# A decoder trunk on one core: the dense stage waits for 96 sums of the second gathered tile, and the first two tiles keep the old row ring

## The chip, the cores and the metric

The kernel runs on one core of a Trainium2 chip. A core has five engines, each working through its own list of instructions in order: TensorE (PE in the profile) multiplies matrices, VectorE (DVE) and ScalarE (ACT) work element by element, GpSimd (POOL) issues the indirect DMAs here, SyncE (SP) issues the plain ones. An instruction that has to wait holds up all that stands behind it on its engine. The metric is the time of one execution on the device in microseconds, lower is better. The kernel before takes 3243.36 us, the median of three runs (3237.42 to 3247.24).

## The reference

The kernel computes one layer of a decoder trunk for 1024 prompt tokens and 32 sample tokens (8 sequences of 4) of width 1024, all in float32. First come mixers (a matrix memory, a spatial gating, a pooling) with a projection in, a projection out and a layer norm. The part that this case is about is the feed-forward that follows, a PEER layer: each token picks 8 heads x 16 of 16384 experts, and each expert is one row of `peer_u` and one row of `peer_v`:

```
s1, i1 = top_k(scores[:, :, 0], 16); s2, i2 = top_k(scores[:, :, 1], 16)
top_s, top_pos = top_k(s1[..., :, None] + s2[..., None, :], 16)   # of 256 pairs, per head
g = softmax(top_s)
act  = gelu(einsum('nd,nhkd->nhk', x2, peer_u[idx]))     # 128 rows of 1024 per token
out  = einsum('nhk,nhkd->nd', g * act, peer_v[idx])      # 128 rows of 1024 per token
y = layer_norm(ALPHA * x1 + g2 * out) * ln2_g + ln2_b
```

## The kernel before, in words

The 1024 prompt tokens are eight tiles of 128, numbered 0 to 7, and the sample tokens are a ninth, numbered 8 (`NT`). They take two ways through the PEER layer.

**Gathered tiles** are 0, 1, 6, 7 and the sample (`GATHERED`, 544 tokens' worth of steps: 4 x 128 and 32). For each step GpSimd issues one indirect DMA (`gather`, L1267 to L1272) that brings 128 rows of 1024 floats, one to a partition, 0.524 MB. `u_items` does this with `peer_u`: the rows of the k-th expert of all 128 tokens, which VectorE multiplies with x2 and sums into a column of `sv` (L1297, in the text also "product"). The index is cast on VectorE from the choice of the experts, 16 columns at a time (L1293, `ii`). After 128 products `finish` makes the coefficients (`cT_`) and the transposed indices (`iT`). `v_items` then does one token per step: its 128 rows of `peer_v` are multiplied on TensorE with an expanded coefficient column (`cexp`, VectorE L1344, one per eight tokens, in a ring of two) and go into a PSUM tile `acc` (L1354; in the text a "sum"; a pair of tokens is eight matmuls in the trace). After a tile's last token comes its finish: `finish_tile` (L1434) before the dense stage, `g_finish` (L1408) in it.

The rows land in two rings of six slots: `rows` from the start, `rows2` for `peer_v` as soon as that scope exists. `rows2` is opened when the text of the dense stage begins, in memory that the scopes `build` and `front` give back (L1476 to L1483).

**Dense tiles** are 2 to 5 (`DENSE`). They compute all 16384 experts for 512 tokens. In the build stage `g_weights` turns the chosen experts into a table: VectorE makes pair tables `ab` (L1041 to L1044, ring of two), ScalarE scales six columns of each (L1046), TensorE multiplies them (`pgm`, L1053), ScalarE copies the result (`gs`, L1056), and SyncE writes it to memory (`G_d`, L1060). `g_pre` beside it does 32 of the 128 score chunks ahead of time. Then the dense stage (`g_dense`, L1095) walks the experts: 24 matmuls `psd` (L1066) for each of the 96 remaining chunks, and 256 groups of 12 matmuls `po` (L1173). ScalarE and VectorE split each incoming table into two half-precision parts (`us`, L1119 and L1120; `vs`, L1136 and L1137), make the coefficients (`act`, `coef`, L1156 to L1164) and add up the outputs (`acc`, L1182).

**What sets the order.** The text of the kernel is produced by generators (`g_main`, `g_gates`, `g_pre`, `g_gather`, and so on), which `run` (L107) takes in turn by rough costs that each yield gives; a generator can wait for a key, such as `("weights", t)` or `"chosen"`, which another adds to `ready`. `g_main` waits for the tables, the choices and the pre-scores before it opens the dense stage (L1471 to L1477). Instructions also carry a priority, gathers a higher one (`AHEAD_S`, `AHEAD_U`, `AHEAD_V`), and a scheduler that simulates the program fixes from text and priorities the order of each engine's list. On the chip only these lists and the semaphores between them count. `g_gather` (L1565) alternates between the `peer_u` steps of one tile and the `peer_v` steps of the tile before it.

Of the kernel before, what the change touches and what calls it, by code (L numbers as in the profile page):

```python
# [44 lines left out]
)  # L45
NROW = 6
NROW2 = 6
MB = 2.78
GATHERED = (0, 1, 6, 7, NT)
DENSE = (2, 3, 4, 5)  # L50
# [27 lines left out]
def kernel(ctx: ExitStack, tc: tile.TileContext, A, O):  # L78
# [236 lines left out]
    ready = set()  # L315
# [948 lines left out]
                            channel_multiplier=0)  # L1264
    coef = {}

    def gather(table, idx):  # L1267
        own = table == "peer_v" and "rows2" in cur
        s = cur["rows2" if own else "rows"].tile("row", (P, D), F32, NROW2 if own else NROW)
        nc.gpsimd.indirect_dma_start(out=s[:], out_offset=None, in_=A[table],  # L1270
                                     in_offset=bass.IndirectOffsetOnAxis(ap=idx, axis=0))
        return s  # L1272
# [51 lines left out]
    def v_items(t):  # L1324


        smp = t == NT
        cT_, iT = coef[t]
        pv = [psum.tile([P, 512], F32, name=f"acc{e}", tag=f"acc{e}", bufs=1) for e in range(2)]
        nj = 8 if smp else 32  # L1330
        hold = {}
        for j in range(nj):
            for q in range(4):

                def step(j=j, q=q):
                    if j % 2 == 0 and q == 0:
                        ce_ = hold["c"] = cur["rows"].tile("cexp", [P, 2, 4, 32], F32, 2)
                        if smp:
                            cv = cT_[:, 4 * j:4 * j + 8].rearrange("p (j q) -> p j q", q=4)
                            dv = delta[:, :, 32 - 4 * j:64 - 4 * j].rearrange("p (j q) c -> p j q c", q=4)  # L1340
                        else:
                            cv = cT_.rearrange("p (q j) -> p j q", q=4)[:, j:j + 2, :]
                            dv = delta[:, 0:2, 32 - j:64 - j].unsqueeze(2).to_broadcast([P, 2, 4, 32])
                        V.tensor_tensor(out=ce_, in0=cv.unsqueeze(3).to_broadcast([P, 2, 4, 32]), in1=dv, op=ALU.mult)  # L1344
                    tok = 4 * j + q if smp else 32 * q + j
                    hold[q % 2] = gather("peer_v", iT[:, tok:tok + 1]), hold["c"][:, j % 2, q, :]
                    if q % 2 == 0:
                        return lambda: None
                    rows = hold[0], hold[1]

                    def add(b, e):
                        g = 32 * (q - 1 + b ^ 2 * e)
                        s, l = rows[b]
                        return mm(pv[e][g:g + 32, :], lhsT=l, rhs=s[:, e * 512:e * 512 + 512], start=(j == 0),  # L1354
                                  stop=(j == nj - 1), skip_group_check=True)

                    def use():
                        first = add(1, 0)
                        with tc.issue_after(first.ins):
                            add(1, 1)  # L1360
                            add(0, 0)
                            add(0, 1)
                    return use
                yield step

        def finish():
            src = pv
            if smp:
                src = []
                f = cur["rows"].tile("row", (P, D), F32, NROW)  # L1370
                fs = [f[:, 0:512], f[:, 512:1024]]
                for e in range(2):
                    (S.activation(fs[e], pv[e], AF.Copy) if e else V.tensor_copy(fs[e], pv[e]))
                yield 0, 1.2, 0
                for e in range(2):
                    b = bank("pfold")
                    mm(b[:NS], lhsT=fold, rhs=fs[e], start=True, stop=True)
                    src.append(b)
                yield 1.8, 0, 0
            if R:  # L1380
                yield from g_finish(t, NS if smp else P, src)
            else:
                finish_tile(t, NS if smp else P, src)
        yield finish
# [78 lines left out]
    def g_main():  # L1463
        yield from g_ada(0)
        load_consts()
        for ts in PASSES:
            yield from g_first(ts)
        cur["proj"].close()
        cur["build"] = Scope("build")
        ready.add("build")  # L1470
        for t in DENSE:  # L1471
            yield from wait(("weights", t))
        yield from wait("chosen")
        yield from wait("pre")
        for t in (NT - 1, NT):
            yield from wait(("y", t, 0))  # L1476
        flush(0)  # L1477
        cur["build"].close()
        cur["front"].close()
        ready.add("dense")  # L1480
        cur["dense"] = Scope("dense")
        dense = g_dense(cur["dense"])
        cur["rows2"] = Scope("rows2", "right")  # L1483
        cur["fin"] = Scope("fin2")
        load_rows()
        yield from dense
# [76 lines left out]
    def g_gather():  # L1563
# [6 lines left out]
        while todo or us or vs or done:  # L1570
            if us is None and todo and (todo[0], 0) in ready and len(done) < 2:
                t = todo.pop(0)
                us, iu = list(u_items(t)), 0
                nu = len(us) - 1
            if vs is None and done:
                vs, iv = list(v_items(done[0])), 0
                nv = len(vs) - 1
            need = None
            if us:
                need = ("routed", t) if iu == nu else (t, 7 if t == NT else iu // 16)  # L1580
            if us and need in ready and (not vs or iu * nv <= 1.4 * (iv - HOLD.get(t, 0) * nv) * nu):
                if iu == nu:
                    flush(0)
                    sooner(AHEAD_F, us[-1])
                    us = None
                    done.append(t)
                    continue
                pend.append((AHEAD_U, sooner(AHEAD_S, us[iu])))
                iu += 1
                c = 0, 1.14, 1.46  # L1590
            elif vs:
                if iv == nv:
                    flush(0)
                    end = vs[-1]()
                    while (x := sooner(AHEAD_F, lambda: next(end, None))):
                        yield x
                    vs = None
                    done.pop(0)
                    continue
                if R and iv >= nv - 24 and iv % 4 == 0:  # L1600
                    if iv == nv - 24:
                        soon = g_ahead(done[0])
                    next(soon, None)
                pend.append((AHEAD_V, sooner(AHEAD_S, vs[iv])))
                iv += 1
                c = 0.43, 0, 1.46
            else:
                yield from wait(need or (todo[0], 0))
                continue
            flush(LAG)  # L1610
            yield c
# [111 lines left out]
```

## Time and profile before

| | |
|---|---|
| median of three runs | 3243.36 us (3237.42 to 3247.24) |
| the profiled execution | 3252.89 us, span 3251.2 us |
| mean granted TensorE clock | 0.902 of full speed |
| TensorE busy | 2748.0 us, 85% of the span |
| VectorE busy | 2202.4 us, 68% |
| GpSimd busy | 1293.1 us, 40% |
| ScalarE busy | 929.6 us, 29% |
| moved by DMA | 962.24 MB, mean 296 GB/s |

Times in the trace count from the start of the span. The busy share of an engine is an average over stages of different kinds. The stretches that the text uses are: the front of the kernel to 1143 us; the last projections and choices to 1360; the build stage to 1668; the dense stage from 1676 to 3092, when the last `po` group is through; and the last gathers to the end.

### The profile page before, as it was taken

How to read it: one execution, taken by the hardware profiler on the slowest of the kernel's cores; microseconds unless marked ns; L12 is line 12 of the kernel's file. 1: busy time of each engine (PE TensorE's matmuls, PEld its weight loads, DVE VectorE, ACT ScalarE, POOL GpSimd, SP SyncE). 2: the span in 40 equal slices, each digit the busy share in tenths (PEclk: the TensorE clock that was granted, in tenths of full speed). 3: DMA queues.
4: the chain of work that ended last, by engine and by line, in shares of the span. 5: the costliest groups of instructions: out<-in, count | busy, mean ns of one | idle time of the engine just before them, and what ended most of it. 6: DMA issues, size and time to landing. Idle time of an engine off the chain costs nothing.

```text
span 3251.2 us, 44766 instructions
## 1 busy us (share of the span) xinstructions
PE 2748.0 (85%) x16366; PEld 1410.6 (43%) x16366; DVE 2202.4 (68%) x5756; ACT 929.6 (29%) x1618; POOL 1293.1 (40%) x1096
## 2 busy tenths in 40 slices
PE   6888984487976888987479999999999998999955
PEld 3447952344654366753343344333344343334300
DVE  2443998867688669777644687777677787777622
ACT  3413243112111124445762222222222222222100
POOL 0000366545445400000013555756465665554564
PEclk8988997687978999989679999999999999999955
DMA  8744798899998844423558999999899999999897
GB/s 296 245 174 138 284 345 292 292 325 312 323 333 291 318 162 141 153 84 137 209 222 317 384 390 353 383 356 399 307 389 368 391 388 363 369 354 353 298 344 257
DMA packets 368993, 962.24 MB, mean 296 GB/s; under 512 B 36757, under 2 KB 114708, under 8 KB 364668
## 3 DMA queue, kind: packets, MB, share of 16 engines
q0 software_dynamic: 156672, 570.49, 47.3%
q1 hardware_dynamic: 212100, 388.89, 34.3%
q8 instruction: 128, 2.10, 0.3%
q14 instruction: 93, 0.76, 0.1%
HBM read 890.30 MB, written 69.02 MB: 295 GB/s over the span
## 4 chain that ended last, share of the span: by engine, by line
PE 50%; DVE 12%; DMA 11%; ACT 4%; issue 3%; POOL 1%; SPq 0%; POOLq 0%; ACTq 0%; DVEq 0%
PE po L1173 18%; PE psd L1066 16%; PE acc L1354 6%; PE pqr L880 4%; DMA row<-in_peer_v,iT 4%; DMA v<-in_peer_v 3%; PE py L808 2%; DVE row L1297 2%; ACT gs L1056 1%; DMA row<-in_peer_u,ii 1%; POOL row L1270 1%; DMA G_d<-gs 1%; DMA wo<-in_w_o 1%; ACT ab L1046 1%; DVE us L1084 1%
## 5 line engine op out<-in xcount | busy, mean ns | idle before, releaser
L1270 POOL DMA_INDIRECT row<-in_peer_v,iT x544 | 631.2, 1160 | 1140.8 <-DVE us L1120 549.0
L1270 POOL DMA_INDIRECT row<-in_peer_u,ii x544 | 659.6, 1212 | 759.6 <-DVE ii L1293 315.9
L1066 PE MATMUL psd<-xd,us 128*128 128x512 f16 x3072 | 719.2, 385 | 29.9 <-ACT us L1083 22.2
L1173 PE MATMUL po<-vs,coef 128*128 128x512 f16 x3072 | 707.8, 380 | 32.2 <-ACT vs L1136 27.1
L1297 DVE SCALAR_TENSOR_TENSOR row<-row,x2u 128x1024 f32<-128x1024 f32 x544 | 656.1, 1216 | 103.2 <-DMA row<-in_peer_u,ii 89.7
L1173 PEld LDWEIGHTS <-coef 128*128 128x128 f16 x3072 | 291.3, 98 | 470.0 <-issue 127.3
L1066 PEld LDWEIGHTS <-us 128*128 128x128 f16 x3072 | 297.4, 99 | 432.0 <-issue 69.9
L1354 PE MATMUL acc<-row,cexp 128*32 128x512 f32 x2176 | 341.8, 690 | 119.2 <-DMA row<-in_peer_v,iT 106.3
L880 PE MATMUL pqr<-x2T,wpq 128*128 128x128 f32 (+1 forms) x2304 | 284.5, 284 | 2.5 <-DVE CT_s L711 0.9
L880 PEld LDWEIGHTS pqr<-x2T,wpq 128*128 128x128 f32 x2304 | 277.2, 200 | 9.0 <-DVE CT_s L711 1.7
L1182 DVE SCALAR_TENSOR_TENSOR acc<-po,scale,acc 128x512 f32<-128x512 f32 x248 | 182.9, 747 | 99.2 <-PE po L1173 90.3
L1156 ACT ACTIVATE act<-psd,scale 128x512 f32<-128x512 f32 x96 | 65.8, 685 | 617.3 <-PE psd L1066 524.8
L1158 DVE SCALAR_TENSOR_TENSOR act<-act,scale,g 128x512 f32<-128x512 f32 x128 | 96.1, 751 | 164.9 <-ACT act L1156 135.1
L1137 DVE SCALAR_TENSOR_TENSOR vs<-v,vs 128x1024 f16<-128x1024 f32 x128 | 155.6, 1219 | 56.6 <-ACT vs L1136 47.6
L1354 PEld LDWEIGHTS acc<-row,cexp 128*32 128x32 f32 x2176 | 48.3, 114 | 292.8 <-DMA row<-in_peer_v,iT 161.2
L1136 ACT ACTIVATE vs<-v 128x1024 f16<-128x1024 f32 x128 | 132.5, 1047 | 142.9 <-DMA v<-in_peer_v 117.8
L1053 PE MATMUL pgm<-ab 128*128 128x128 f16 x1024 | 98.9, 253 | 83.2 <-DVE ab L1043 43.9
L808 PE MATMUL py<-wo,Y 128*128 128x512 f32 (+1 forms) x288 | 144.6, 653 | 21.4 <-DMA wo<-in_w_o 12.4
L1120 DVE SCALAR_TENSOR_TENSOR us<-u,us 128x1024 f16<-128x1024 f32 x96 | 117.3, 1222 | 46.9 <-ACT us L1119 45.3
L1163 ACT ACTIVATE coef<-act 128x512 f16<-128x512 f32 x128 | 79.8, 624 | 201.9 <-DVE act L1158 174.7
L1056 ACT ACTIVATE gs<-pgm 128x256 f32<-128x256 f32 x256 | 124.1, 633 | 40.8 <-PE pgm L1053 25.6
L279 PEld LDWEIGHTS <-w 128*128 128x128 f16 x2160 | 123.1, 100 | 24.8 <-issue 21.7
(337 smaller groups left out, 2856.6 us busy)
## 6 DMA issues: line engine op xcount, KB each, us to landing
v<-in_peer_v SPq DMA_DIRECT2D x128, 512.0 KB
u<-in_peer_uT SPq DMA_DIRECT2D x96, 512.0 KB
wpq<-in_w_pq SPq DMA_DIRECT2D x64, 512.0 KB
G_d<-gs SPq DMA_DIRECT2D x32, 1024.0 KB
g<-G_d SPq DMA_DIRECT2D x32, 1024.0 KB
wada<-in_w_ada SPq DMA_DIRECT2D x48, 512.0 KB
wf<-in_w_in SPq DMA_DIRECT2D x44, 512.0 KB
wo<-in_w_o SPq DMA_DIRECT2D x32, 512.0 KB
```

The costliest lines, as they stand in the source:

```text
L279: mm(out, lhsT=x if cs is None else y, rhs=y if cs is None else x, start=(i + k == 0), stop=(i == len(ps) - 1 and k == KD - 1))
L808: mm(py[t, e][:ns[t]], lhsT=Y_[t][:, k + j, :ns[t]], rhs=w[:, j, :], start=(k + j == 0), stop=(k + j == KD - 1))
L880: mm(pq[:, i * P:i * P + ns[t]], lhsT=w[:, k, :], rhs=X2[t][:, k, :ns[t]], start=(k == 0), stop=(k == KD - 1))
L1056: S.activation(gs[e][:, :, t0:t0 + 4].rearrange("p c t -> p t c"), pg[:, :, 64 * e:64 * e + 64], AF.Copy)
L1066: mm(ps, lhsT=us[a][:, k, :], rhs=xd[:, :, b, k, :], start=(m == 0), stop=(m == 23))
L1136: S.activation(vs[:, 0], v, AF.Copy, scale=SV)
L1137: V.scalar_tensor_tensor(out=vs[:, 1], in0=v, scalar=SV, in1=vs[:, 0], op0=ALU.mult, op1=ALU.subtract)
L1173: mm(po, lhsT=d[:, a, i * P:(i + 1) * P], rhs=vs[:, b, c % 2, :], start=(m == 0), stop=(m == 3 * GROUP - 1))
L1182: V.scalar_tensor_tensor(out=a, in0=po, scalar=scale[:, 3:4], in1=a, op0=ALU.mult, op1=ALU.add)
L1270: nc.gpsimd.indirect_dma_start(out=s[:], out_offset=None, in_=A[table], in_offset=bass.IndirectOffsetOnAxis(ap=idx, axis=0))
L1297: V.scalar_tensor_tensor(out=s, in0=s, scalar=1.0, in1=x2, op0=ALU.mult, op1=ALU.mult, accum_out=sv[:, k:k + 1])
L1354: return mm(pv[e][g:g + 32, :], lhsT=l, rhs=s[:, e * 512:e * 512 + 512], start=(j == 0), stop=(j == nj - 1), skip_group_check=True)
```

## The change

A constant `AMPLE` is added. The generator of the main text waits for one more key, `"ample"`, before it opens the dense stage; `g_gather` adds the key when it has put 96 steps of tile 1's `peer_v` into the text. `gather` no longer looks whether `rows2` is open: the caller says which ring it wants, and the `peer_v` rows of tiles 0 and 1 go to `rows`, those of 6, 7 and the sample to `rows2`.

```
@@ -45,6 +45,7 @@
 NROW = 6
 NROW2 = 6
+AMPLE = 96
 MB = 2.78
@@ -1264,8 +1265,7 @@
-    def gather(table, idx):
-        own = table == "peer_v" and "rows2" in cur
+    def gather(table, idx, own=False):
         s = cur["rows2" if own else "rows"].tile("row", (P, D), F32, NROW2 if own else NROW)
         nc.gpsimd.indirect_dma_start(out=s[:], out_offset=None, in_=A[table],
                                      in_offset=bass.IndirectOffsetOnAxis(ap=idx, axis=0))
@@ -1343,7 +1343,7 @@
-                    hold[q % 2] = gather("peer_v", iT[:, tok:tok + 1]), hold["c"][:, j % 2, q, :]
+                    hold[q % 2] = gather("peer_v", iT[:, tok:tok + 1], t not in GATHERED[:2]), hold["c"][:, j % 2, q, :]
@@ -1472,6 +1472,7 @@
             yield from wait(("weights", t))
         yield from wait("chosen")
         yield from wait("pre")
+        yield from wait("ample")
         for t in (NT - 1, NT):
             yield from wait(("y", t, 0))
@@ -1603,6 +1604,8 @@
                 pend.append((AHEAD_V, sooner(AHEAD_S, vs[iv])))
                 iv += 1
+                if done[0] == GATHERED[1] and iv == AMPLE:
+                    ready.add("ample")
                 c = 0.43, 0, 1.46
```

In the lists the change moves instructions at three places. Line numbers of the changed kernel are higher by one from L49 to L1266.

The first is GpSimd's list after the 256th `peer_u` step, the last of tile 1. Before, the rest of tile 0's `peer_v` rows follow, then a run of `peer_u` and `peer_v` rows in fives:

```order
L1270 DMA row<-in_peer_v,iT 128x1024
L1270 DMA row<-in_peer_u,ii 128x1024 x6
L1270 DMA row<-in_peer_v,iT 128x1024 x45
L1270 DMA row<-in_peer_u,ii 128x1024 x5
L1270 DMA row<-in_peer_v,iT 128x1024 x5
```

In the changed kernel 37 rows end tile 0 (its 128th), and the next `peer_u` row is tile 6's first:

```order
L1270 DMA row<-in_peer_u,ii 128x1024 x2
L1270 DMA row<-in_peer_v,iT 128x1024 x37
L1270 DMA row<-in_peer_u,ii 128x1024
L1270 DMA row<-in_peer_v,iT 128x1024
L1270 DMA row<-in_peer_u,ii 128x1024
L1270 DMA row<-in_peer_v,iT 128x1024
```

Behind it the rows of tile 6's `peer_u` and of tile 1's `peer_v` alternate.

The second is VectorE's list in the last third of the build stage. Before, the pair tables stand by themselves:

```order
L1041 TENSOR_TENSOR ab<-iota_106,fx 128x2048
L1042 TENSOR_TENSOR ab<-iota_106,fx 128x2048
L1043 TENSOR_TENSOR ab<-ab,fx 128x2048 x2
L1044 TENSOR_TENSOR ab<-ab,fx 128x1280 x2
L1041 TENSOR_TENSOR ab<-iota_106,fx 128x2048
L1042 TENSOR_TENSOR ab<-iota_106,fx 128x2048
```

In the changed kernel the products of tile 6 (L1297) stand between them:

```order
L1297 SCALAR_TENSOR_TENSOR row,sv<-row,x2u 128x1024
L1044 TENSOR_TENSOR ab<-ab,fx 128x2048
L1138 SCALAR_TENSOR_TENSOR vs<-v,vs 128x1024
L1297 SCALAR_TENSOR_TENSOR row,sv<-row,x2u 128x1024 x2
L1045 TENSOR_TENSOR ab<-ab,fx 128x1280
L1297 SCALAR_TENSOR_TENSOR row,sv<-row,x2u 128x1024
L1042 TENSOR_TENSOR ab<-iota_106,fx 128x2048
L1043 TENSOR_TENSOR ab<-iota_106,fx 128x2048
```

There are 79 such products between the cast of tile 6's first index and the last pair table, where before there was none.

The third is VectorE's list where the last gathered sums stand. Before, that is behind everything of the dense tiles; the first two rows end the last dense tile:

```order
L360 TENSOR_TENSOR mv<-vy,vy_25117 128x1
L785 SCALAR_TENSOR_TENSOR acc_14544<-acc_14544,mv,r_ln_b 128x1024
L1344 TENSOR_TENSOR cexp<-cT__23093,delta 128x256 x4
L1344 TENSOR_TENSOR cexp<-cT__25294,delta 128x256 x2
L1420 TENSOR_TENSOR row<-row,r_g_14531 128x1024
```

In the changed kernel it is inside the dense stage, behind the 187th of the 256 `po` groups:

```order
L1121 SCALAR_TENSOR_TENSOR us<-u,us 128x1024
L1165 TENSOR_TENSOR coef<-act,coef 128x512
L1183 SCALAR_TENSOR_TENSOR acc_15617<-po,scale,acc_15617 128x512
L1344 TENSOR_TENSOR cexp<-cT__19789,delta 128x256 x8
L1344 TENSOR_TENSOR cexp<-cT__22401,delta 128x256 x2
L1420 TENSOR_TENSOR row<-row,r_g_15605 128x1024
```

Ten `cexp` in a row, each for eight tokens, take the place of six, and 69 `po` groups come behind them. TensorE's list has 106 tokens' sums in one piece there; before it had 88 behind the last `po` group.

## Rows read from the trace of the kernel before

**Rows 1.** The page, parts 1 and 2: busy time; busy tenths in 40 slices.

```profile
PE 2748.0 (85%) x16366; PEld 1410.6 (43%) x16366; DVE 2202.4 (68%) x5756; ACT 929.6 (29%) x1618; POOL 1293.1 (40%) x1096
...
PE   6888984487976888987479999999999998999955
...
POOL 0000366545445400000013555756465665554564
```

**Rows 2.** The waits of GpSimd: us in total, times, longest.

```profile
POOL row L1270 <- DVE us L1120: 549.0, 1, 549.0
```

**Rows 3.** Timeline of GpSimd: start, us, instruction, idle before and releaser.

```profile
1135.53 0.94 POOL L1270 DMA_INDIRECT row<-in_peer_u,ii  x1 [1.39 <-DVE row L1297]
1685.46 0.94 POOL L1270 DMA_INDIRECT row<-in_peer_v,iT  x1 [548.99 <-DVE us L1120]
1686.70 0.94 POOL L1270 DMA_INDIRECT row<-in_peer_v,iT  x1 [0.30 <-issue]
```

**Rows 4.** Windows by stage: header, then busy time of each engine.

```profile
core 0: us, PE busy (x) PEld busy (x) DVE busy (x) ACT busy (x) POOL busy (x), PEclk, DMA share, GB/s
1143.00:1360.00 217.00, 196.36 (x1396) 148.65 (x1394) 167.30 (x773) 81.58 (x168) 0.00 (x0) 0.95 0.43 147
1360.00:1545.00 185.00, 149.31 (x1013) 92.30 (x1012) 134.94 (x570) 87.88 (x172) 0.00 (x0) 0.95 0.33 117
1545.00:1668.00 123.00, 60.18 (x554) 50.65 (x551) 81.20 (x89) 93.25 (x236) 0.00 (x0) 0.64 0.48 185
1676.00:3092.00 1416.00, 1376.81 (x6856) 546.05 (x6854) 1004.97 (x1474) 377.41 (x491) 790.49 (x661) 0.99 0.98 362
3092.00:3251.00 159.00, 85.92 (x356) 9.72 (x356) 39.65 (x116) 2.38 (x4) 83.23 (x83) 0.54 0.84 301
```

**Rows 5.** Waits of TensorE, the first of 1685 to 3095, the second of 3092 to 3251.

```profile
PE po L1173 <- ACT vs L1136: 27.1, 12, 4.3
...
PE acc L1354 <- DMA row<-in_peer_v,iT: 58.9, 42, 4.0
```

**Rows 6.** Timeline of TensorE: dense stage, a pair of tokens, the ends.

```profile
1675.96 16.32 PE L1066 MATMUL psd<-xd,us 128*128 128x512 f16 x72
...
1701.50 1.07 PE L1354 MATMUL acc<-row,cexp 128*32 128x512 f32 x8
...
3090.58 1.25 PE L1173 MATMUL po<-vs,coef 128*128 128x512 f16 x5
...
3233.25 1.93 PE L1354 MATMUL acc<-row,cexp 128*32 128x512 f32 x8 [1.94 <-DMA row<-in_peer_v,iT]
```

**Rows 7.** Windows with gathers beside choosing, beside projections, and alone; columns as in group 4.

```profile
350.00:500.00 150.00, 137.16 (x1300) 99.72 (x1298) 141.21 (x471) 57.83 (x89) 87.06 (x67) 0.97 0.96 349
700.00:1136.00 436.00, 351.19 (x2110) 214.59 (x2108) 329.07 (x1267) 68.79 (x153) 212.66 (x182) 0.86 0.90 315
3100.00:3230.00 130.00, 75.85 (x316) 8.48 (x320) 22.36 (x67) 1.78 (x3) 77.86 (x79) 0.52 0.95 341
```

**Rows 8.** Tile 6's index casts on VectorE: shortest, median, longest ns; first, last start.

```profile
L1293 DVE CAST ii<-rt x4: 168/168/176, 1360.2 to 1360.4; 128x16 int32<-128x16 f32 x4
```

**Rows 9.** Timeline of VectorE: `cexp`, two products, a half-row operation.

```profile
1138.33 0.42 DVE L1344 TENSOR_TENSOR cexp<-cT__6780,delta 128x256 f32<-128x256 f32 x1
...
1140.91 1.22 DVE L1297 SCALAR_TENSOR_TENSOR row<-row,x2u 128x1024 f32<-128x1024 f32 x1
...
1142.18 1.23 DVE L1297 SCALAR_TENSOR_TENSOR row<-row,x2u 128x1024 f32<-128x1024 f32 x1
...
1152.07 0.69 DVE L816 TENSOR_TENSOR z<-py,g 128x512 f32<-128x512 f32 x1 [6.73 <-PE py L808]
```

**Rows 10.** TensorE in the dense stage, of `acc`, `psd` and `po` in this order.

```profile
1676.00:3092.00 1416.00, 197.08 (x1472) 0.99 0.98 362
...
1676.00:3092.00 1416.00, 539.68 (x2304) 0.99 0.98 362
...
1676.00:3092.00 1416.00, 707.82 (x3072) 0.99 0.98 362
```

More of the change, by code (lines that the diff above doesn't have):

```diff
@@ L47 @@
 NROW2 = 6
+AMPLE = 96
 MB = 2.78
@@ L1265, with gather @@
     coef = {}
-    def gather(table, idx):
-        own = table == "peer_v" and "rows2" in cur
+    def gather(table, idx, own=False):
         s = cur["rows2" if own else "rows"].tile("row", (P, D), F32, NROW2 if own else NROW)
@@ L1345, in step @@
                     tok = 4 * j + q if smp else 32 * q + j
-                    hold[q % 2] = gather("peer_v", iT[:, tok:tok + 1]), hold["c"][:, j % 2, q, :]
+                    hold[q % 2] = gather("peer_v", iT[:, tok:tok + 1], t not in GATHERED[:2]), hold["c"][:, j % 2, q, :]
                     if q % 2 == 0:
@@ L1474, in g_main @@
         yield from wait("pre")
+        yield from wait("ample")
         for t in (NT - 1, NT):
@@ L1605, in g_gather @@
                 iv += 1
+                if done[0] == GATHERED[1] and iv == AMPLE:
+                    ready.add("ample")
                 c = 0.43, 0, 1.46
```

## The prediction

> **What bounds the kernel now.** The page's first two parts come first. TensorE is busy 85% of the span and its digits are 8 and 9 almost to the end, while GpSimd shows eight zeros in mid-kernel, so whole gathers are being held back there [rows 1]. The waits of GpSimd name the hole: one wait of 549.0 us [rows 2]. The timeline gives its place: the last row of `peer_u` for tile 1 is issued at 1135.53, the next row, one of `peer_v`, at 1685.46, with the start of the dense stage [rows 3]. The row is tile 0's 89th; it has to go into the new ring `rows2`, whose memory becomes free only there. So 88 of 544 `peer_v` rows and 256 of 544 `peer_u` rows are behind us when the dense stage begins.
>
> The windows cut the rest into stages [rows 4]: 1143 to 1360 is paced by TensorE (196.4 of 217 us busy), 1360 to 1668 by VectorE (134.9 of 185 us) and by the chain through ScalarE (93.3 of 123 us), 1676 to 3092 by TensorE (1376.8 of 1416 us), and from 3092 nothing but rows for the last sums is left. There TensorE waits 58.9 us for landings [rows 5]. The last 88 tokens take from 3092 to 3235 [rows 6], 143 us or 1.62 us each; then 16 us of finishing.
>
> **The change, part by part.** The sum is made against the profiled span, 3251.2 us (its run took 3252.9). The median of the three runs is 3243.4, so a result in profile time is multiplied by 0.997.
>
> *Until 1143 us: nothing.* Every engine's order is word for word the same until token 89's sum.
>
> *1143 to 1360: +10 us.* Tokens 89 to 128 of tile 0 now use the old ring and go at once. Their 40 sums stand among the projections. Two tokens take 1.07 us [rows 6], so 40 take 21 us on an engine with 20.6 us idle in the stretch. Between 0 and 21 I take the middle. The 21 MB of rows go beside 147 GB/s of other traffic, and make 244 GB/s of it, against 341 in the tail [rows 7]. Then GpSimd meets the first `peer_u` row of tile 6, which needs an index that VectorE casts at 1360 [rows 8]; that row now stands ahead of tile 1's sums, and all of them wait behind it in GpSimd's queue. So some 150 us of the 549 stay empty.
>
> *1360 to 1668: +56 us, the term that decides.* Between that cast and the last pair table (`ab`) of the build, VectorE's order now has 79 products of `peer_u` rows, 7 `cexp`, and the finishing of tile 0. Products follow each other at 1.27 us (1140.91, 1142.18), `cexp` costs 0.42, and the 13 or so half-row operations of the finish are near the 0.69 of a half-row `z` [rows 9]: 100.3 + 2.9 + 9 = 112 us. VectorE was busy 216 us of these 308 [rows 4], so it needs at least 328: +20 us if it never idles. From the other side: beside gathers VectorE was 75% busy from 700 to 1136 (329.1 of 436 us), which would make 437 us, +129. In 350 to 500, where choosing and products also share it, it was 94% busy [rows 7]: 349 us, +41. I take 90%, nearer to that stretch: 364 us. It is not less packed because the choosing is VectorE alone; it is not 94% because the second half is a chain of VectorE, ScalarE, TensorE and back with two buffers, and products that wait for a landing now stand between its links. Behind each such product the next `ab` waits, behind that ScalarE's scaling and TensorE's `pgm`.
>
> The other costs of the moved steps are put at nothing. Some 58 sums here are 31 us on a TensorE that idles 98 us. The finish of tile 0 adds a dozen loads to SyncE's queue, behind the last projection weights. The transfers are close to being a bound themselves: 44 MB so far (117 and 185 GB/s [rows 4]) and 137 rows of 0.524 MB are 116 MB, 340 us at the tail's 341 GB/s, within the 364; a smaller growth than 32 us has no room for them.
>
> Whether GpSimd's gathers take VectorE time is read from 350 to 500: VectorE was busy 141.2 us and GpSimd 87.1 us of the same 150 [rows 7], so the two mostly overlap, and nothing is charged. Only a gather's own length speaks for a conflict: 1.30 us there (87.1 over 67) against 0.99 in the tail (77.86 over 79). If in the build the two excluded each other after all, 137 gathers at 0.94 us [rows 3] would add 129 us to the 328: 457 us, +149 instead of +56, and the kernel would take 3358. The Trainium skill states such a rule ("SBUF — State Buffer", section "SBUF: two separate sides"): VectorE and GpSimd have a pair of ports in common, which is not shared but locked, and whoever starts first holds it for its whole instruction. By that rule, taken for every gather, the time is the 3358 of the sentence before; the trace agrees no further than the 1.30 us.
>
> *Dense stage: -76 us.* It starts with 190 tokens done instead of 88. Before, 368 tokens were summed in it (1472 matmuls, four each, 197.1 us [rows 10]), 0.535 us each. Now 354 remain, but the order puts 106 of them, all that is left at that point, in one piece behind 187 of the 256 output groups (`po`); 248 lie among the dense matmuls, 120 fewer: -64 us. The `po` and `psd` matmuls, 707.8 and 539.7 us, are the same. TensorE idled 39 us, 27.1 of them for `v` that came late beside the gathers [rows 5]; the last three tenths now run without gathers: -12 us. That the transfers set the pace (362 GB/s [rows 4]) I leave out, because TensorE is 97% busy.
>
> *The piece of 106 sums: +176 us, where the tail was -143 us.* VectorE's order shows the same: ten `cexp` in a row with nothing of the dense stage between them, each waiting for the sums before it. So both engines stand still for dense work while rows land. The ring holds six rows, so no more than six can be there in advance, as in the tail. 106 at the tail's 1.62 us are 172 us; 4 us for the dense chain to restart. The tail at the end is gone, its finishing is replaced by that of the last dense tile: about 16 us each, 0.
>
> The tail's 1.62 us a row is what the rows show of gathers alone. The Trainium skill ("DMA: Bandwidth & Descriptors", section "Anatomy of one DMA — SWDGE (gpsimd) path") gives 2.0 us fixed and the bytes at 436 GB/s; with the fixed part hidden by the ring, an estimate from it is 1.20 us a row, 127 us for the piece, and the kernel at 3220. The tail does not show that pace.
>
> Sum: 3251 + 10 + 56 - 76 + 176 - 143 = 3274 us in the profile, 3265 as a median. What was a tail is now a standstill two thirds into the dense stage, so the gathers that were moved earlier buy back only their sums, and they are paid for on VectorE where it had least to spare.
>
> **Rivals.**
> 1. *VectorE packs at 94 to 100%.* Growth 20 to 41 us instead of 56: 3229 to 3250. For it: the 94% of 350 to 500 held for 150 us. Against it: ScalarE's 93.3 of 123 us.
> 2. *The build stage does not grow, so the kernel gets faster.* Place: 1360 to 1668. The products would all fall into VectorE's 92 idle us, and its instructions would overlap where I add them. Price: 56 us less, 3209. It decides once the growth is under 24 us. Against it: 328 us of VectorE work in 308.
> 3. *The piece runs at GpSimd's issue pace.* Rows issued back to back are 1.24 us apart (1685.46, 1686.70 [rows 3]): 131 us, 41 less, 3224. For it: nothing else is loading then. Against it: the tail was just as alone and took 1.62.
> 4. *The build stage goes at the 75% of 700 to 1136*, because products wait for landings: +129 there, 3338. If gathers and VectorE exclude each other, as worked out above, 3358.
>
> **How the numbers follow.** Forecast 0.50, rival 1 0.21, rival 2 0.09, rival 3 0.08, rival 4 0.08 and its second case 0.04. The forecast's own range is 3254 to 3310: a share of 94% down to 81%. The bound for no change is 0.3%, 3234 to 3253; about that much can be told from nothing. Slower: 0.50 + 0.12 = 0.62; same: rival 1, 0.21; faster: rivals 2 and 3, 0.17. The range 3212 to 3325 leaves out most of rival 4 with its second case, and about half of rival 2.
>
> **What the new profile would show.** GpSimd's wait of 549 us is replaced by one of about 150 us that ends with the cast near 1370. The first dense `psd` piece (72 matmuls at 1675.96 [rows 6]) moves to about 1742. Some 170 us before the last 69 `po` groups, TensorE's digits fall to about half at the low clock, as in the tail now, and VectorE's to almost none. The last instructions are those of a dense tile and no `pfold`. Wrong would be: the dense stage starting before 1710, no standstill, or a standstill under 140 us; then the kernel is not slower. A start after 1790 would be rival 4.

## The result, and the profile after

The changed kernel takes 3298.35 us, the median of four runs (3289.84 to 3302.50), against 3243.65 for the kernel before (four runs): a ratio of 1.0167, 95% interval 1.0142 to 1.0193. A second set of runs, on another occasion, gave 3298.31 (five runs) against 3253.05 (nine runs): 1.0140, interval 1.0118 to 1.0162. It is slower, as forecast, but by 45 to 55 us where 22 were forecast.

The page of the changed kernel, parts 1 and 2, to be laid beside [rows 1]:

```profile
PE 2763.4 (84%) x16366; PEld 1415.8 (43%) x16366; DVE 2205.8 (67%) x5763; ACT 938.7 (29%) x1618; POOL 1320.7 (40%) x1096
...
PE   6888983587976798987657999999999999559996
...
POOL 0000366535444530045754454655665553650000
```

GpSimd's zeros in mid-kernel, six there (the prediction counted eight), have shrunk to two, TensorE's 5s have moved from the end to slices 35 and 36, and GpSimd is empty for the last four slices. The busy times are the same within 2.2%: the work has only been moved. GpSimd's timeline, in answer to [rows 3], shows the hole as forecast, 143 us instead of 549. It ends with the cast of tile 6's first index at 1385.6; the releaser that the row names is only the last semaphore event before it.

```profile
1242.66 0.94 POOL L1270 DMA_INDIRECT row<-in_peer_v,iT  x1 [0.31 <-PE pt L843]
1386.56 0.94 POOL L1270 DMA_INDIRECT row<-in_peer_u,ii  x1 [142.96 <-PE ps L886]
1387.80 0.94 POOL L1270 DMA_INDIRECT row<-in_peer_v,iT  x1 [0.30 <-issue]
```

TensorE's timeline, in answer to [rows 6]: the first dense matmul, the standstill's beginning and a pair in it, the `po` behind it.

```profile
1761.75 7.20 PE L1067 MATMUL psd<-xd,us 128*128 128x512 f16 x27
...
2793.51 1.92 PE L1354 MATMUL acc<-row,cexp 128*32 128x512 f32 x16
2799.30 1.94 PE L1354 MATMUL acc<-row,cexp 128*32 128x512 f32 x8 [3.87 <-DMA row<-in_peer_v,iT]
...
2963.68 3.73 PE L1174 MATMUL po<-vs,coef 128*128 128x512 f16 x12
```

The windows by stage, with the columns of [rows 4]: to the index cast, build, dense stage, standstill, dense stage again, end.

```profile
1143.00:1386.00 243.00, 215.36 (x1551) 151.49 (x1549) 171.33 (x784) 83.95 (x172) 39.44 (x37) 0.94 0.60 214
1386.00:1762.00 376.00, 259.91 (x1824) 152.49 (x1824) 324.43 (x858) 190.53 (x426) 223.01 (x145) 0.81 0.91 332
1762.00:2793.00 1031.00, 1011.10 (x5009) 404.08 (x5008) 720.46 (x1047) 289.50 (x373) 543.73 (x459) 0.99 0.98 358
2793.00:2964.00 171.00, 101.37 (x432) 11.73 (x431) 19.60 (x42) 2.56 (x5) 96.28 (x101) 0.57 0.90 320
2964.00:3262.00 298.00, 298.00 (x1378) 134.95 (x1377) 176.32 (x224) 92.44 (x115) 0.00 (x0) 1.00 0.39 123
3262.00:3288.00 26.00, 0.68 (x4) 0.10 (x1) 22.13 (x79) 0.00 (x0) 0.00 (x0) 0.58 0.20 81
```

In the standstill TensorE's mean granted clock is 0.57 of full speed (of its two levels, 1.2 and 2.4 GHz, mostly the lower; a pair of tokens takes 1.94 us there instead of 1.07), VectorE does 20 us of work in 171, and the rows come at 320 GB/s; behind it nothing is gathered any more, and the transfers fall to 123 GB/s while TensorE is full. With a second profile of both kernels (spans 3245.7 and 3292.9) the prediction's sum can be checked term by term:

| term | forecast | first pair | second pair |
|---|---|---|---|
| to the cast of tile 6's indices | +10 | +25.4 | +27.8 |
| cast to first dense matmul | +56 | +60.4 | +62.2 |
| dense stage without the standstill | -76 | -85.2 | -80.1 |
| standstill of 106 sums | +176 | +170.2 | +172.2 |
| from the last `po` to the end | -143 | -133.9 | -134.9 |
| sum | +23 | +36.9 | +47.2 |

The first pair of profiles shows less than the 55 us between the medians, because the first profile of before was 9 us above its median and the first of after 8.5 below.

### The profile page after: what moved, and what is told of

The parts are those of the page before. It is cut to its first block, busy times and chain, and to the rows that moved or that the text cites. A ratio compares the mean times of both kernels' runs of the same rounds, so it can differ in the third digit from the quotient of the medians.

```text
span 3288.1 us, 44890 instructions
## 1 busy us (share of the span) xinstructions
PE 2763.4 (84%) x16366; PEld 1415.8 (43%) x16366; DVE 2205.8 (67%) x5763; ACT 938.7 (29%) x1618; POOL 1320.7 (40%) x1096
## 4 chain that ended last, share of the span: by engine, by line
PE 48%; DMA 12%; DVE 9%; issue 7%; ACT 2%; POOL 1%; SPq 0%; POOLq 0%; DVEq 0%; ACTq 0%
PE po L1174 19%; PE psd L1067 16%; DMA row<-in_peer_v,iT 6%; PE acc L1354 6%; DMA row<-in_peer_u,ii 3%; PE py L809 2%; DVE row L1297 2%; PE pqr L881 2%; POOL row L1270 1%; DMA G_d<-gs 1%; ACT gs L1057 1%; DMA v<-in_peer_v 1%; DMA act<-sd_d 0%; PE pvp L280 0%; DMA wo<-in_w_o 0%
## 5 line engine op out<-in xcount | busy, mean ns | idle before, releaser
L1270 POOL DMA_INDIRECT row<-in_peer_u,ii x544 | 679.8, 1250 | 987.2 <-DVE ii L1293 312.5
L1270 POOL DMA_INDIRECT row<-in_peer_v,iT x544 | 638.7, 1174 | 608.9 <-PE acc L1354 369.1
L1297 DVE SCALAR_TENSOR_TENSOR row<-row,x2u 128x1024 f32<-128x1024 f32 x544 | 657.2, 1215 | 161.9 <-DMA row<-in_peer_u,ii 148.7
L1354 PE MATMUL acc<-row,cexp 128*32 128x512 f32 x2176 | 362.3, 720 | 176.4 <-DMA row<-in_peer_v,iT 175.5
L1183 DVE SCALAR_TENSOR_TENSOR acc<-po,scale,acc 128x512 f32<-128x512 f32 x248 | 183.2, 746 | 71.0 <-PE po L1174 70.5
L809 PE MATMUL py<-wo,Y 128*128 128x512 f32 (+1 forms) x288 | 141.5, 641 | 18.2 <-DMA wo<-in_w_o 11.5
L1054 PEld LDWEIGHTS <-ab 128*128 128x128 f16 x1024 | 83.2, 118 | 102.3 <-issue 55.4
```

The lines of the kernel that those rows point to most:

```text
L809: mm(py[t, e][:ns[t]], lhsT=Y_[t][:, k + j, :ns[t]], rhs=w[:, j, :], start=(k + j == 0), stop=(k + j == KD - 1))
L1054: mm(pg[:, j, :], lhsT=ab[:, 0, t4 + j, :], rhs=ab[:, 1 + e, t4 + j, :], start=(e == 0), stop=(e == 1))
L1183: V.scalar_tensor_tensor(out=a, in0=po, scalar=scale[:, 3:4], in1=a, op0=ALU.mult, op1=ALU.add)
L1297: V.scalar_tensor_tensor(out=s, in0=s, scalar=1.0, in1=x2, op0=ALU.mult, op1=ALU.mult, accum_out=sv[:, k:k + 1])
```

## Experiments

The kernels nosums, norows, neither, halfrows, noprods, nocons and tworings were run once each, so each gives the figures of one execution; the other changed kernels have four to ten runs.

**The same kernel again.** No edit.

> The changed kernel once more, to see which stage differs between executions. By the two profiles the change costs 36.9 us of span (3251.2 to 3288.1), by the medians 54.7 us. Theory A: the price is in three places, which are the same in every execution: 40 sums in the TensorE-paced stretch (+25 us to the index cast of tile 6), the build stage (+60 us from that cast to the first dense matmul), and a standstill of 106 sums (+170) that costs more than the lost tail gives back (-134) and the dense stage saves (-86); the 18 us between the two figures is spread of single executions. Then the second profile shows each of these within 8 us, and a median of 3290 to 3302. Theory B: one stage, the build most of all, is longer by 15 us or more in a typical execution.

> The kernel before once more, for a second profile beside those of after. Theory A: the same stages within 8 us each (index cast 1360, first dense matmul 1676, last po 3092), and the spread of the times is spread of all stages. Theory B: one stage differs by 15 us or more.

Measured: the cast at 1389.6 and 1361.8, the build (from the cast to the first dense matmul) 378.0 and 315.8 us, the standstill 172.2. No stage is more than 9 us off its first profile: what differs between executions is spread over all of them.

**Is the standstill the loss?** Two ways to take it out: `AMPLE = 32`, and `AMPLE = 96` with `("dense", {"g_gather": 1.2})` instead of 0.8.

> AMPLE is 32 instead of 96. The lists up to 160 po groups are those of the changed kernel; the difference is that the last 90 sums stand among the dense matmuls, the last one behind po group 224, and not 106 in one piece. Theory A: the standstill is the loss. Its 170 us become 106 x 0.535 = 57 us, and the time falls from 3298 to about 3185, faster than before; the build stage stays as long as with 96. Rival (landings): rows that are spread over the dense matmuls make TensorE wait for each landing, as 20 waits of 27.8 us did in this stage; then half or less of the 113 us is gained, 3240 or more.

> The wait at 96, as in the changed kernel, and the planner's factor for gathers in the dense stage 1.2 instead of 0.8. All that moves is the last piece: no standstill, the last sum behind po group 224, as with AMPLE 32. Theory: the price of the wait is the standstill alone, and the planner's pace can take it back: 3185 to 3200. Rival: the wait itself costs; 3230 or more.

Measured: 3191.62 us, ratio 0.9807 (0.9784 to 0.9830), and 3192.51, 0.9849 (0.9806 to 0.9892), both faster than the kernel before. In ample32 the first dense matmul is at 1769.3, where after_again has it at 1767.7, and the last `po` is through at 3164.0 instead of 3267.5: the same front and build, and some 104 us less behind them. dense12 keeps the wait at 96 and is as fast, so the wait has no price of its own: the standstill is the loss. Why the wait makes one is read from the generators and shown by no run alone: the dense text seems to have been written out while 106 gathers were left, so that these came in one piece. dense12, where the planner takes gathers faster, fits that.

**The ring change without the wait.** The line `yield from wait("ample")` is taken out.

> The ring change alone, without the wait. Its lists have 186 sums ahead of the first po where the changed kernel has 190, 76 products in the build instead of 80, and no piece of sums. Theory A: the ring choice alone moves the gathers into the build, and the wait does nothing but shift the text so that the standstill arises: about 3185, as ample32, with the dense stage starting within 8 us of 1762. Rival: the wait is what holds the dense stage back; then it starts 20 us or more earlier than 1762.

Measured: 3307.79 us, 1.0181 (1.0152 to 1.0210). Both theories fall: no standstill, the dense stage starts at 1776.9, and still it is slow, since the dense stage lasts 1493 us. TensorE's `acc` busy time there, of ringonly and then of ample32 (us, busy, clock, DMA share, GB/s), and a stretch of ringonly's timeline:

```profile
1777.00:3270.00 1493.00, 295.30 (x1448) 1.00 0.88 313
```

```profile
1769.00:3164.00 1395.00, 193.01 (x1432) 0.99 0.91 331
```

```profile
2005.21 1.04 PE L1354 MATMUL acc<-row,cexp 128*32 128x512 f32 x2
2006.19 0.39 PE L1067 MATMUL psd<-xd,us 128*128 128x512 f16 x1
2006.51 1.04 PE L1354 MATMUL acc<-row,cexp 128*32 128x512 f32 x2
...
2055.56 1.07 PE L1354 MATMUL acc<-row,cexp 128*32 128x512 f32 x8
```

Almost the same number of sums costs 102 us more. The eight matmuls of a pair of tokens, four instructions on four different strips of the array, take 1.07 us side by side; one instruction of them alone between two dense matmuls takes 1.04. In ringonly's list 126 of them stand alone, in its trace 120. The follow-up keeps the ring change and raises `AHEAD_V` from 2000 to 8000; its edit also raises `AHEAD_F`, the priority of a gathered tile's finish, from 4000 to 8000:

> The ring change alone, as ringonly, with AHEAD_V at 8000 instead of 2000, so that the matmuls of the sums are put into the list ahead of dense ones. In ringonly 126 matmul instructions of the sums stood alone between dense matmuls, in this one none. Theory A: a sum's instruction that stands alone takes 1.04 us, where the four of a pair of tokens side by side take 1.07 together; that is what made ringonly's dense stage 1493 us long for the same work that took 1395 in ample32. Then this kernel takes 3180 to 3195 against 3308. Rival: ringonly was slow because without the wait the dense loads and the gathers collide; then it stays above 3270.

Measured: 3239.22 us, 0.9956 (0.9939 to 0.9972). From the first dense matmul to the last `po` it needs 1405 us instead of 1493, with `acc` back at 194.3 us for the same 1448 matmuls, while `psd` and `po` cost what they did (537 and 707 us, against 539 and 711): the mechanism is shown. The forecast time was missed by 45 us. The dense stage starts at 1801.8 instead of 1776.9, since the cast came 18 us later and the build took 401 us instead of 394; and it is 11 us longer than that of ample32.

**What makes the front late?** nosums leaves out matmuls, norows the 40 rows, neither both; halfrows, further below, halves the bytes. The core of norows:

```
+                    if t == 0 and j >= 22:
+                        hold[q % 2] = hold["old"][q % 2], hold["c"][:, j % 2, q, :]
+                    else:
                         hold[q % 2] = gather("peer_v", iT[:, tok:tok + 1], t not in GATHERED[:2]), ...
```

> The changed kernel without the matmuls of 36 of the 40 sums that moved out of tile 0 and of 120 of tile 1's 128 (left out of the result); their rows are still gathered, and the last piece of 108 sums stays. Theory A for the projection stretch (the sums are simply added to a full TensorE): the index cast of tile 6 comes at 1366 or earlier instead of 1386 to 1390. Rival (21 MB of rows slow the weight loads): it stays at 1385. For the build: if the sums between the table matmuls carry part of the 60 us, the stretch from the cast to the first dense matmul falls from 376 to 350 or less; if products alone carry it, it stays at 370 or more.

> The changed kernel, where the last 40 peer_v rows of tile 0 are not gathered; their sums are kept and read two rows that are already there (other values, left out of the result). The cast of tile 6's indices came at 1360 and 1362 in the kernel before, at 1377 to 1398 (mean 1389) in seven profiles with these rows and sums, at 1381 twice with the rows alone. Rows theory (the 21 MB delay the weight and x loads): 1370 or earlier. Sums theory: 1380 or later. Additive: the sums' 21 us of matmuls, 1381, if no row helps.

> As norows, and the matmuls of 36 of the 40 sums left out too. If rows and sums between them make the front late, the cast is back at 1360 to 1364. If it is later than 1368, something else that moved there does it: the finish of tile 0 with its dozen loads, or the order itself.

The index cast (first and last start) in after_again, nosums, norows and neither:

```profile
L1293 DVE CAST ii<-rt x4: 168/168/175, 1389.6 to 1389.8; 128x16 int32<-128x16 f32 x4
```

```profile
L1293 DVE CAST ii<-rt x4: 166/168/176, 1381.0 to 1381.2; 128x16 int32<-128x16 f32 x4
```

```profile
L1293 DVE CAST ii<-rt x4: 166/166/175, 1366.2 to 1366.5; 128x16 int32<-128x16 f32 x4
```

```profile
L1293 DVE CAST ii<-rt x4: 167/169/174, 1362.5 to 1362.7; 128x16 int32<-128x16 f32 x4
```

With neither rows nor sums the front is the old one (1360.2 and 1361.8). Sums without rows cost 5 us, rows without sums 20. With both, the cast came at 1376.8 (dense12) to 1397.6 (halfprod) in the profiles with this front, so 1366.2 and 1362.5 lie outside this scatter, and the 1381.0 of nosums (1380.7 in nocons, below) within it: the rows are most of the delay. Half the bytes (halfrows, below) brought it to 1375.8, too near the scatter to count. At the end little of it is left: norows took 3289.57 us and neither 3287.67, since the build took 391 and 390 us there. Where rows are gathered, other loads land later. One of VectorE's waits, of nosums from 1143 to 1381 and of the kernel before from 1143 to 1360:

```profile
DVE z L823 <- DMA x<-in_x: 8.3, 1, 8.3
```

```profile
DVE z L822 <- DMA x<-in_x: 0.6, 2, 0.4
```

TensorE's two waits for the `z` that come out of such steps rise with it, from 11.6 us in the kernel before (11.5 in neither) to 23.2 in nosums. That accounts for some 12 of the 20 us; where the rest arises was not traced.

**What makes the build long?** Halved products, half the bytes, no products, and almost nothing that reads the rows.

> The changed kernel, with the products of tile 6 over 512 of the 1024 columns (the other half of its scores is left out); all rows are gathered as before. The 78 products in the build then take about 0.65 us instead of 1.22 each, 45 us less of VectorE. Theory A (VectorE sets the growth of the build): the stretch from the index cast to the first dense matmul, 376 us with whole products and 316 without any, falls to 330 to 340, and the time from 3298 to about 3258. Rival (landings and the chain through ScalarE and TensorE set it): it stays at 370 or more, and the time at 3290 or more. Between them: both.

> The changed kernel, where the rows that moved into the choosing and build stages (tile 6's peer_u, tile 1's peer_v and the last 40 peer_v rows of tile 0) are gathered with half the bytes, from a table seen as twice as many rows of 512 (other values, left out of the result); tile 6's products run over 512 columns, the sums keep all their matmuls. The lists hold more in the build than those of the changed kernel: 113 products and 82 sums instead of 80 and 62. Theory C (transfers set the build: it moved 125 MB in 376 us, 123 in 371 with half products, 132 in 389 without sums, always 332 to 339 GB/s): bytes fall to about 100 MB, and the stretch from the cast to the first dense matmul to 340 us or less. Rival (each waiting instruction in the in-order lists lengthens the chain, whatever the bytes): 365 us or more. In the front the cast comes at 1375 or earlier if transfers made the delay there, at 1385 or later if not.

> The changed kernel, where the first 112 products of tile 6 read x2 over 8 columns instead of the gathered row (their scores are left out of the result); all rows are still gathered, and all sums are there. From the cast to the first dense matmul the changed kernel needs 376 to 378 us (five profiles), halved products 371, no sums 389, half the bytes 404 with more gathers, the kernel before 316. Theory D (a product holds VectorE's list until its row has landed, and through the ring of six slots that products and sums have in common holds the sums too): without products 345 us or less. Rival (transfers): 365 or more. Rival (sums on TensorE's list do it): 360 to 375.

> Both left out: those products, and the matmuls of 36 of the last 40 sums of tile 0 and of 120 of tile 1's; the rows of all of them are still gathered, over 135 in the build. Nothing there waits for a landing any more. Theory D: the build is back near the 316 us of the kernel before, at most 330; the transfers cost nothing by themselves. Rival (transfers): 360 or more, as in the changed kernel. In the front the cast comes at 1376 to 1398 in seven profiles of kernels with these 40 sums or their rows, 1360 and 1362 before: by 1366 if the sums' matmuls make it late, after 1376 if their rows do.

The build from the cast to the first dense matmul, by windows, with the columns of [rows 4]: of halfprod, halfrows, nosums, noprods, nocons.

```profile
1398.00:1768.00 370.00, 252.28 (x1810) 150.63 (x1811) 281.07 (x854) 189.50 (x425) 188.13 (x142) 0.81 0.89 332
```

```profile
1376.00:1780.00 404.00, 276.60 (x1920) 156.24 (x1919) 305.07 (x930) 190.16 (x427) 256.35 (x201) 0.81 0.76 253
```

```profile
1381.00:1770.00 389.00, 231.09 (x1607) 152.55 (x1607) 331.06 (x869) 190.60 (x425) 241.86 (x159) 0.75 0.91 339
```

```profile
1387.00:1740.00 353.00, 244.17 (x1824) 147.67 (x1824) 232.49 (x694) 189.66 (x427) 185.34 (x146) 0.85 0.94 354
```

```profile
1381.00:1774.00 393.00, 231.13 (x1604) 151.84 (x1604) 230.03 (x688) 190.28 (x425) 236.68 (x198) 0.75 0.99 386
```

halfprod refutes VectorE's time as the cause: 43 us less work on VectorE (324.4 to 281.1), and the build is 6 us shorter; its median of 3283.76 is 15 below that of the changed kernel, not 40 (the profile is of the slowest of its four runs). noprods shows that products cost 24 of the 61 us as a whole; halved ones wait for the same landings (VectorE's waits for rows are 49 us there, 33 in the changed kernel). nosums gives no sign that the sums' matmuls cost the rest: without them the build is 12 us longer, but it also holds 159 gathers instead of 145. nocons decides nothing: without readers GpSimd issued 198 gathers, and the DMA engines were 99% busy. halfrows refutes the bytes as the only cause: 102 MB, 76% busy, and 404 us, but the scheduler had put 201 gathers into it. There VectorE waits 72.6 us for rows and TensorE 60.0:

```profile
DVE row L1298 <- DMA row<-in_peer_u,ii: 72.6, 41, 5.0
```

```profile
PE acc L1355 <- DMA row<-in_peer_v,iT: 60.0, 18, 10.2
```

What is shown: no version with gathers in the build took under 352 us, against 316 without any; 24 us hang on products. How the other 37 divide stays open, between full DMA queues (354 GB/s in noprods), waits for landings in the lists, and a third thing that no run isolates: VectorE's work holds up the gathers themselves. While VectorE is idle a gather takes GpSimd 0.94 us; in the changed kernel's build it takes 1.54 on average (223.01 us over 145), in noprods 1.27. The longest, and the VectorE instruction before which VectorE first pauses again:

```profile
1625.52 10.75 POOL L1270 DMA_INDIRECT row<-in_peer_v,iT  x1 [0.30 <-issue]
```

```profile
1635.81 1.22 DVE L1297 SCALAR_TENSOR_TENSOR row<-row,x2u 128x1024 f32<-128x1024 f32 x1 [0.36 <-DMA row<-in_peer_u,ii]
```

For the first 9.9 us of this gather VectorE had no gap; then it paused for 0.36 us, and 0.8 us after the pause began the gather was through.

**Without products in the build.** Tile 6's `peer_u` rows use the new ring and start with the dense stage, `peer_v` rows keep the old one.

```
-            if us is None and todo and (todo[0], 0) in ready and len(done) < 2:
+            if us is None and todo and (todo[0], 0) in ready and len(done) < 2 and (todo[0] in GATHERED[:2] or "dense" in ready):
-            s = gather("peer_u", ii[:, k:k + 1])
+            s = gather("peer_u", ii[:, k:k + 1], t not in GATHERED[:2])
-                    hold[q % 2] = gather("peer_v", iT[:, tok:tok + 1], t not in GATHERED[:2]), ...
+                    hold[q % 2] = gather("peer_v", iT[:, tok:tok + 1]), ...
```

> The wait stays at 96; tile 6's peer_u steps begin only with the dense stage, peer_u rows of tiles 6, 7 and the sample use the new ring, peer_v rows always the old one. So the build holds 256 sums instead of 190 and none of tile 6's products. Theory A (VectorE sets the build's growth): the 60 us shrink to 5 to 15, while 44 more sums among the projections cost 44 x 0.6 = 27 us in the stretch before; the dense stage starts near 1740 and, with 288 sums left and no standstill, lasts 1360: about 3125. Rival (transfers or ScalarE set it): the gathers in the build are about as many (128 instead of 137), so the growth stays near 60, the dense stage starts near 1790 and the time is 3175.

> swap96 with AHEAD_V 4000, as a candidate for the best version: fewer sums stand alone between other matmuls (11 runs of one to three instead of 14), and more of tile 1's sums (74 instead of 44) stand among the projections rather than between the table matmuls. If the chain of the build pays more for a sum than the projections do, 3150 to 3165; if the projections pay as much, 3170 to 3180, the same as swap96.

Measured: 3172.61 us, 0.9763 (0.9722 to 0.9804), the lowest median of all, and 3175.96, 0.9788 (0.9746 to 0.9831), no different. The build of swap96 took 360 us with 85 rows and 90 sums, and the dense stage began at 1758.1, between the 1740 of theory A and the 1790 of the rival: the time is the rival's, but not by its terms. Theory A, that products set the growth, fails again. So does a growth by full DMA queues alone: in this build, by windows as above, the DMA engines were 71% busy, and still it is 44 us longer than before.

```profile
1398.00:1758.00 360.00, 266.50 (x1968) 154.54 (x1967) 233.16 (x696) 190.57 (x429) 114.04 (x85) 0.85 0.71 263
```

**The pace of the standstill.** Every second row of tile 7 and of the sample goes to the old ring.

> The changed kernel, with every second peer_v row of tile 7 and of the sample in the old ring, so that the standstill has twelve slots instead of six (it is two pieces here, of 32 and 60 sums). Theory (the standstill runs at the pace of the transfers, 328 GB/s at 93% busy DMA engines): 1.55 to 1.65 us a row as with six slots. Rival (it runs at the latency of six slots): 1.25 us a row, GpSimd's own pace.

TensorE's `acc` there (us, busy, clock, DMA share, GB/s), tworings and then the changed kernel:

```profile
2850.00:2935.00 85.00, 56.88 (x240) 0.80 0.96 358
```

```profile
2796.00:2957.00 161.00, 93.83 (x400) 0.55 0.94 335
```

60 rows in 85 us are 1.42 us each, against 100 in 161, 1.61: between the two theories. Six more slots buy 0.19 us a row, at a higher granted clock too; GpSimd issues rows 1.24 us apart for long stretches there, and what is left over are pauses of 2 to 4 us, with the DMA engines 96% busy. The run took 3262.23.

## Why the prediction was wrong

- *Direction, places and shape* were right: the hole of about 150 us that ends with the cast, the later dense stage, the standstill behind the 187th `po` group, the end without `pfold`. The standstill was forecast at 176 us and measured at 170 and 172; it is the loss, since taking it out makes the kernel faster than before. The lower end of the forecast's own range, 3254, does not match the 94% named with it, which gives 3250; nothing hangs on it.
- *The step that failed* is the one on 1143 to 1360: "Between 0 and 21 I take the middle", and "The 21 MB of rows go beside 147 GB/s of other traffic". It priced the sums' matmuls, of which norows shows 5 us, and the rows at nothing; they cost 20 (nosums), in part through later landings of other loads (`x`). On average there was room, as forecast: 214 GB/s and DMA engines 60% busy; the delay came all the same. Measured +25 and +28 instead of +10. It is not a loss by itself, though: with rows and sums gone (neither) the dense stage starts at 1752.3, only 9 and 15 us before the changed kernel's 1761.8 and 1767.7, and dense12, which has both, starts it at 1754.6. Front and build share one delay of +86 and +90 us, where the prediction added two terms to 66; this is most of what it missed.
- *The build* was forecast at +56 and came at +60 and +62, but for the wrong reason. VectorE was busy 324 us of 376, 86%, close to the 90% of the text; yet halving the products turned busy time into waiting. So +56 was near by luck. The transfers, set aside as "within the 364", are not the whole answer either, as swap96 shows; 24 us hang on products and the rest is open. The second case of rival 4, VectorE lengthened by every gather, is not seen; what is seen is the other direction, GpSimd's gathers held up while VectorE works (above), and the 1.30 us that the prediction noted was its sign. The groups of VectorE that make one piece of the pair tables, before from 1143 to 1676 without a gather beside them, and after from 1386 to 1762 beside 145 gathers (count, busy, mean ns, idle before):

```profile
L1043 DVE TENSOR_TENSOR ab<-ab,fx 128x2048 f16<-128x2048 f16 x30 | 36.2, 1217 | 0.3
```

```profile
L1044 DVE TENSOR_TENSOR ab<-ab,fx 128x2048 f16<-128x2048 f16 x25 | 30.3, 1216 | 0.1
```

- *The dense stage* saved 85 and 80 us, not 76. *The end* costs 26 us behind the last `po`, not 16: two dense tiles are normalised there after it.
- Rival 3's pace of 1.24 us a row is not reached over the whole piece even with twelve slots; neither is the 1.20 that was estimated from the Trainium skill ("DMA: Bandwidth & Descriptors", section "Anatomy of one DMA — SWDGE (gpsimd) path").

## What to carry to other kernels

Work that is moved to where engines are idle brings its transfers along: price what its transfers do to the loads that the stage waits for, not only the average bandwidth. Look in the new order for a long piece of one kind of work; it stands still at the pace of its ring, and one number of a planner can make or remove it. Filling idle engines in mid-kernel was worth 0.4 to 2.4% here, and only in the orders with neither a standstill nor sums that stand alone.

## What the runs showed of the hardware

VectorE holds up indirect gathers; that gathers hold up VectorE is not seen. In the changed kernel's profile the 215 gathers that find VectorE idle take 0.94 to 0.95 us on GpSimd; in the build, with VectorE 86% busy, the mean is 1.54 and the longest 10.75, while VectorE's own 128x2048 operation keeps its 1216 ns. Not every VectorE instruction does it: 36 gathers meet only the sums `acc<-po,scale,acc` (L1183), which read PSUM, and take 0.94 to 0.95.

Four matmul instructions on four 32-column strips of the array take 1.07 us when they follow each other, and 1.04 us each when a dense matmul stands between them: in ringonly that alone cost about 100 us, with TensorE busy for 1475.0 of the 1493 us. A busy share near 100% doesn't tell whether matmuls overlap; the busy time of one tile for the same count does (193.0 against 295.3 us).
